# Inverse square roots in the attention and scan part of a decoder layer: starting value on ScalarE, one Newton step on VectorE

## The chip, the cores and the metric

The kernel runs on one core of a Trainium2 chip. The metric is the time of the device for one execution in microseconds (us), the median of several runs. The core has five engines that take their instructions in order, each from a queue of its own, and wait for each other by semaphores: TensorE (PE, with its weight loads as PEld), VectorE (DVE), ScalarE (ACT), GpSimd (POOL) and SyncE (SP, which here only issues DMAs).

## The reference

One layer of a decoder is computed for two groups of requests that share the weights: a prompt of 1024 tokens, and 8 sequences with 4 new tokens each and 4096 cached positions. The parts that the change touches:

```python
def rms_norm(x, g):
    xf = x.astype(jnp.float32)
    y = xf * lax.rsqrt(jnp.mean(xf * xf, axis=-1, keepdims=True) + NORM_EPS)
    return (y * g.astype(jnp.float32)).astype(x.dtype)

def mla_keys(c, w_uk, kn_g):
    return rms_norm(jnp.einsum('...tr,rhd->...thd', c, w_uk), kn_g)

# decoder_layer, in the middle of it
    gdn_out, new_conv, new_s = gdn_mixer(...)      # ends in rms_norm(o, norm_g) * silu(z)
    qn, qr, c, kr = mla_project(...)
    ctx = mla_attend(qn, qr, c, kr, lp['mla_w_uk'], lp['mla_kn_norm'])
    mix = jnp.concatenate([gdn_out, mla_out.astype(gdn_out.dtype)], axis=-1) @ lp['w_out']
```

For the sample group, `mla_attend` makes keys from all 8 x 4096 cached latents (128 numbers each, 8 heads of 64), and each key of each head is divided by the root of its mean square. These roots, and those of the scan's output, are the ones that the change treats.

## The kernel before

The program is one straight run of instructions, made by a tile scheduler that orders each engine's queue by a simulated time line and by the order in the source; GpSimd's order is fixed by hand in the middle of the layer. Products of large size are made of three fp32r matmuls (high and low halves of the operands, `mm3`, lines 125 to 129), which is why nearly all of TensorE's time stands on lines 127 to 129. The stages follow each other: adaLN and first norm, first SwiGLU up and down (to about 900 us), the mixer's input projections with convolution, norms and the triangular inverses (`mixer_in`, to about 1285 us), the heads (`mixer_heads`, about 1285 to 2010 us), output projection, second SwiGLU.

`mixer_heads` (line 2030) is where the change acts. Three pieces of work are woven together there by `together` (line 2017), in a fixed ratio of their steps:

- `mla_prompt_gen`, the prompt's softmax attention, to about 1694 us: tiles `pS`, `pT`, `pa` on TensorE, `pf` and `phi` on ScalarE (lines 1696, 1699), `plo` on GpSimd.
- `scan_gen` with `gdn_sample`, from about 1680 us on: the gated delta scan of the prompt in 17 dependent steps (tiles `sv`, `S`, `so`), and the same recurrence for the sample tokens as a long run of elementwise operations on GpSimd (tiles `gS`, `gt`, all recorded on line 101). `gdn_out` (line 1356) normalises each of the scan's 8 output tiles and the sample's: 9 calls.
- `sample_gen`, attention of the 8 sample sequences over the cache, through the whole of both stages. For each sequence four pieces of cache come by indirect DMA from GpSimd's queue (`fetch`, tile `ck`, line 635; six buffers for the pieces). Each piece is transposed (`kpt`), split (`khi`, `klo`), multiplied to keys (`kraw`), squared on ScalarE (`ksq`, line 2000) and summed per head on VectorE (`kss`, line 2001). After every half of a sequence the function `half` (line 1823) takes the inverse root of 128 x 128 sums, spreads it (`rx`, line 1836, on ScalarE), transposes it (`psr`) and scales the scores with it (`sc`, line 1849). After the second half `soft` makes the softmax and multiplies it with the pieces (`psc`, line 1883), and only then are four buffers free for the next `fetch`. There are 16 halves.

The inverse root itself is `pow_rs` (line 713): one operation for mean and epsilon (line 717), then `rsqrt` (line 704): a starting value by integer arithmetic on the bits (line 707), then three Newton steps of three operations each (lines 709, 710, 711), all on VectorE: 11 operations in a row that depend on each other. In the listings the tile `pv` holds the argument and the temporary, `rsk` the result in `half` (128 x 128), `ors` the result in `gdn_out` (128 x 8). `norm_sums`, `tok_l2`, `head_norm`, `mla_c_post` and `mla_q_finish` use the same functions in other stages.

Of the kernel before, what the change touches and what calls it, by code (L numbers as in the profile page):

```python
# [11 lines left out]
AF = mybir.ActivationFunctionType  # L12
ALU = mybir.AluOpType
# [7 lines left out]
NP = 1024  # L21
NSEQ = 8
NQ = 4
NS = NSEQ * NQ
NT = NP + NS
NB = 4
BW = NT // NB
# [47 lines left out]
class Banks:  # L75


    def __init__(self, **pools):
        self.pools = pools
# [5 lines left out]
class Kernel:  # L85
    def __init__(self, tc, ins, outs, dbg=None):
        self.tc, self.nc, self.i, self.o = tc, tc.nc, ins, outs
        self.dbg = dbg or (lambda name, ap: None)
        self.ctx = ExitStack()
        self.wcount = 0  # L90
        self.hhi, self.hlo, self.nacc, self.nr = ([None] * NB for _ in range(4))

    def pool(self, name, **kw):
# [610 lines left out]
    def rsqrt(self, y, v, t):  # L704

        nc = self.nc
        nc.vector.tensor_scalar(y.bitcast(I32), v.bitcast(I32), -0.5, float(0x5f3759df), ALU.mult, ALU.add)
        for _ in range(3):
            nc.vector.tensor_tensor(out=t, in0=y, in1=y, op=ALU.mult)
            nc.vector.scalar_tensor_tensor(out=t, in0=t, scalar=-0.5, in1=v, op0=ALU.mult, op1=ALU.mult)  # L710
            nc.vector.scalar_tensor_tensor(out=y, in0=t, scalar=1.5, in1=y, op0=ALU.add, op1=ALU.mult)

    def pow_rs(self, out, ss, n, scale, tp, post=None, bufs=2):

        nc = self.nc
        v = tp.tile([P, 2, n], F32, tag=f"pv{n}", name="pv", bufs=bufs)
        nc.vector.tensor_scalar(v[:, 0], ss, scale, EPS, ALU.mult, ALU.add)
        self.rsqrt(out, v[:, 0], v[:, 1])
        if post is not None:
            nc.vector.tensor_scalar(out, out, post, None, ALU.mult)  # L720

# [159 lines left out]
    def taps(self, m, raw, tp):  # L881

        nc = self.nc
        W = NP + 3 + 7 * NSEQ
        sraw = raw[:, NP + 3:].rearrange("p (s r) -> p s r", r=7)
        nc.scalar.copy(raw[:, 0:3], self.zero3)
        nc.scalar.copy(sraw[:, :, 0:3], self.stT[:, m, :].rearrange("p (s j) -> p s j", j=3))
        nc.gpsimd.tensor_copy(self.ncv[:, m, 0:3], raw[:, NP:NP + 3])
        nc.gpsimd.tensor_copy(self.ncv[:, m, 3:27].rearrange("p (s j) -> p s j", j=3), sraw[:, :, 4:7])
        self.done["n"] += 1  # L890
        y = self.r(tp, [P, NTL * P], "cy")
        n = W - 3
        nc.scalar.activation(y[:, :n], raw[:, 0:n], AF.Copy, scale=self.convw[:, 0, m:m + 1])
        for j in range(1, 4):
            nc.vector.scalar_tensor_tensor(out=y[:, :n], in0=raw[:, j:j + n], scalar=self.convw[:, j, m:m + 1], in1=y[:, :n],
                                           op0=ALU.mult, op1=ALU.add)
        nc.scalar.activation(raw[:, :NP], y[:, :NP], AF.Silu)
        nc.scalar.activation(raw[:, NP:NT].rearrange("p (s q) -> p s q", q=NQ), y[:, NP + 3:W].rearrange("p (s r) -> p s r", r=7)[:, :, 0:4], AF.Silu)
        return raw, y

    def tok_l2(self, yt, post, tp, ps):
# [323 lines left out]
    def proj_z(self, m, tp, ps):  # L1225
        nc = self.nc
        zt = self.r(tp, [P, NT], "zt")
        self.proj(lambda b, pp, mm: nc.scalar.activation(zt[:, b * BW:(b + 1) * BW], pp[:, :BW], AF.Silu), ps)
        nc.scalar.dma_start(out=self.z_d[m], in_=zt)

    def mixer_start(self):
# [798 lines left out]
    def mixer_heads(self):  # L2030
        nc, tc, i = self.nc, self.tc, self.i
        self.mix_tiles()
        self.spare = None
        with tc.tile_pool(reuse_waits="tile", name="mc", bufs=1) as mc:
            raw = mc.tile([P, 3, P], F32, name="mraw")
            for n, src in enumerate(("k_causal", "k_causalT", "k_nident")):
                nc.scalar.dma_start(out=raw[:, n, :], in_=i[src])
            self.k_nident = raw[:, 2, :]
            rnd = mc.tile([P, 3, P], F32R, name="mrnd")
            nc.vector.tensor_copy(rnd[:, 0:2], raw[:, 0:2])  # L2040
            nc.vector.tensor_copy(rnd[:, 2], self.ident)
            self.causal, self.causalT, self.identr = (rnd[:, n, :] for n in range(3))
            self.k_eye8 = mc.tile([104, 8], F32, name="k_eye8")
            nc.scalar.dma_start(out=self.k_eye8[96:104], in_=i["k_eye8"])
            self.g_gdn = self.keep.tile([P, 1], F32, name="g_gdn")
            for r in range(2):
                with nc.allow_non_contiguous_dma(reason="a gain per partition"):
                    nc.scalar.dma_start(out=self.g_gdn[64 * r:64 * r + 64, :], in_=i["gdn_norm"][0].rearrange("(d o) -> d o", o=1))
            with tc.tile_pool(reuse_waits="tile", name="sq", bufs=1, side="right") as sq, tc.tile_pool(reuse_waits="tile", name="psq", bufs=PSQ, space=PSUM) as pq:
                smp = self.sample_gen(sq, pq)  # L2050
                with tc.tile_pool(reuse_waits="tile", name="mpp", bufs=1) as mp, tc.tile_pool(reuse_waits="tile", name="psm", bufs=1, space=PSUM) as ps:
                    with tc.manual_schedule(engines={getattr(mybir.EngineType, e) for e in MX}):
                        self.together([(self.mla_prompt_gen(mp, ps), 1)], (smp, RATIO[0]))
                with tc.tile_pool(reuse_waits="tile", name="se", bufs=1) as se, tc.tile_pool(reuse_waits="tile", name="sc", bufs=1) as sp, tc.tile_pool(reuse_waits="tile", name="pss", bufs=SCB, space=PSUM) as ps:
                    with tc.manual_schedule(engines={getattr(mybir.EngineType, e) for e in MY}):
                        self.together([(self.scan_gen(se, sp, ps, "S"), 1), (self.gdn_sample(sp, ps, "S"), RATIO[2])], (smp, RATIO[1]))
                    for _ in smp:
                        pass
# [199 lines left out]
```

## Time and profile before

| | us |
|---|---|
| median of 3 runs | 2859.01 (2853.66 to 2862.34) |
| the profiled execution | 2863.72 |
| its span, first to last instruction | 2861.9 |
| TensorE busy in the span | 2673.6 |
| VectorE busy | 1766.6 |
| ScalarE busy | 1074.2 |
| GpSimd busy | 1083.2 |

The profile shows one execution. A busy time is the sum of what an engine's instructions took; times of instructions that only wait are not in it. Where a group of instructions is listed, the columns are line, engine, operation, written tile and read tiles, shapes, count, busy time in us and mean of one in ns, and behind the bar the idle time of the engine just before, with what ended it. Stretches are given in us from the start of the span. PEclk is the share of TensorE's full clock that was granted.

### The profile page before, as it was taken

The page shows a single profiled execution, that of the slowest core. Times are in us where ns is not written, and L with a number is a line of the kernel's source. Part 1 is how long each engine was busy: PE and PEld are TensorE (multiplying, and loading weights), DVE is VectorE, ACT ScalarE, POOL GpSimd, SP SyncE. Part 2 cuts the span into 40 slices and gives each one's busy share as a digit, 9 for nine tenths or more (in the row PEclk, how much of TensorE's full clock was granted, in tenths as well). Part 3 has the DMA queues.
Part 4 walks back from the last instruction along what each step waited for, and adds up shares of the span by engine and source line. Part 5 has one row for each costly group of instructions (what it writes and reads, how often), then busy time and mean ns, then how long its engine had stood idle before and what let it go on. Part 6 is the DMA issues. An engine that isn't in the chain of part 4 may idle for free.

```text
span 2861.9 us, 53475 instructions
## 1 busy us (share of the span) xinstructions
PE 2673.6 (93%) x21536; PEld 2462.5 (86%) x21536; DVE 1766.6 (62%) x3490; ACT 1074.2 (38%) x2005; POOL 1083.2 (38%) x1032
## 2 busy tenths in 40 slices
PE   4999999989999897799999988998979999999999
PEld 3888989989999787787877866776979999999999
DVE  7644445465574688847767677777585555546555
ACT  5322223211144443324656664543443333322111
POOL 0222222233352555544434466452433333323331
PEclk7999999999999998898999998987979999999999
DMA  7554353243232473432212144222522222224322
GB/s 272 154 163 134 120 162 105 81 161 106 76 109 77 149 206 117 141 110 78 63 42 58 49 96 114 83 64 53 188 82 82 76 87 71 90 82 167 98 76 69
DMA packets 339490, 308.35 MB, mean 108 GB/s; under 512 B 93865, under 2 KB 282017, under 8 KB 336171
## 3 DMA queue, kind: packets, MB, share of 16 engines
q1 hardware_dynamic: 304837, 246.32, 28.4%
q10 hardware_dynamic: 28262, 37.64, 4.1%
q0 software_dynamic: 6144, 20.98, 2.3%
q8 instruction: 169, 2.77, 0.4%
q14 instruction: 78, 0.64, 0.1%
HBM read 229.29 MB, written 75.59 MB: 107 GB/s over the span
## 4 chain that ended last, share of the span: by engine, by line
PE 42%; DVE 8%; issue 5%; POOL 4%; DMA 2%; ACT 1%; SPq 0%; ACTq 0%; POOLq 0%; DVEq 0%
PE po L128 4%; PE po L129 4%; PE po L127 4%; PE pY L127 2%; PE pY L128 2%; PE pY L129 2%; PE kraw L127 2%; PE pX L127 2%; PE pX L128 2%; PE pX L129 1%; PE pZ L127 1%; PE pZ L129 1%; PE pZ L128 1%; PE kraw L129 1%; PE kraw L128 1%
## 5 line engine op out<-in xcount | busy, mean ns | idle before, releaser
L127 PE MATMUL po<-act,whi 128*128 128x264 f32 x1408 | 402.4, 286 | 6.4 <-DVE x L435 4.7
L129 PE MATMUL po<-act,wlo 128*128 128x264 f32 x1408 | 403.2, 286 | 0.0
L128 PE MATMUL po<-act,whi 128*128 128x264 f32 x1408 | 402.0, 286 | 0.0
L435 DVE SCALAR_TENSOR_TENSOR x<-po,modT,x 128x264 f32<-128x264 f32 (+1 forms) x416 | 195.2, 480 | 238.8 <-PE po L129 238.3
L127 PEld LDWEIGHTS po<-act,whi 128*128 128x128 f32 x1408 | 266.8, 189 | 7.1 <-DVE x L435 4.9
L129 PEld LDWEIGHTS po<-act,wlo 128*128 128x128 f32 x1408 | 266.1, 189 | 0.0
L128 PEld LDWEIGHTS po<-act,whi 128*128 128x128 f32 x1408 | 265.9, 189 | 0.0
L370 POOL TENSOR_TENSOR A<-wg,A 128x512 fp32r<-128x512 f32 x84 | 111.0, 1321 | 372.1 <-ACT A L369 372.1
L127 PE MATMUL pp<-hhi,whi 128*128 128x264 f32 (+1 forms) x768 | 223.9, 292 | 4.5 <-DVE nt L354 3.6
L128 PE MATMUL pp<-hlo,whi 128*128 128x264 f32 (+1 forms) x768 | 223.7, 291 | 0.0
L129 PE MATMUL pp<-hhi,wlo 128*128 128x264 f32 (+1 forms) x768 | 221.8, 289 | 0.0
L2001 DVE TENSOR_REDUCE kss<-ksq 128x8 f32<-128x512 f32 x256 | 173.1, 681 | 69.7 <-ACT ksq L2000 67.7
L127 PE MATMUL pX<-B,A 128*128 128x264 f32 x704 | 203.9, 290 | 10.6 <-ACT B L369 9.7
L111 POOL TENSOR_TENSOR wlo<-wraw,whi 128x1024 fp32r<-128x1024 f32 x39 | 97.7, 2510 | 305.2 <-ACT whi L108 305.2
L2000 ACT ACTIVATE ksq<-kraw 128x512 f32<-128x512 f32 x256 | 152.1, 598 | 162.1 <-PE kraw L129 122.2
L128 PE MATMUL pX<-B,A 128*128 128x264 f32 x704 | 202.9, 288 | 8.9 <-DVE B L370 8.9
L128 PE MATMUL pY<-T,S 128*128 128x264 f32 x704 | 200.7, 285 | 1.6 <-DVE T L370 1.5
L129 PE MATMUL pX<-B,A 128*128 128x264 f32 x704 | 201.6, 286 | 0.0
L127 PE MATMUL pY<-T,S 128*128 128x264 f32 x704 | 200.3, 285 | 0.0
L129 PE MATMUL pY<-T,S 128*128 128x264 f32 x704 | 200.2, 284 | 0.0
L1700 POOL TENSOR_TENSOR plo<-pf,phi 128x512 fp32r<-128x512 f32 (+1 forms) x96 | 97.1, 1017 | 187.4 <-ACT phi L1699 169.7
L108 ACT CAST whi<-wraw 128x1024 fp32r<-128x1024 f32 x60 | 61.8, 1048 | 253.6 <-PE po L128 234.1
(538 smaller groups left out, 8305.1 us busy)
## 6 DMA issues: line engine op xcount, KB each, us to landing
adaw<-ada_w SPq DMA_DIRECT2D x72, 512.0 KB
wraw<-ffn_wi SPq DMA_DIRECT2D x46, 512.0 KB
act_d<-cc SPq DMA_DIRECT2D x88, 264.0 KB
wraw<-ffn_wo SPq DMA_DIRECT2D x44, 512.0 KB
wg<-ffn_wi SPq DMA_DIRECT2D x42, 512.0 KB
araw<-act_d ACTq DMA_DIRECT2D x160, 132.0 KB
x_d<-x SPq DMA_DIRECT2D x12, 1056.0 KB
wraw<-w_in SPq DMA_DIRECT2D x23, 512.0 KB
```

Of the source, the lines that this page charges most:

```text
L108: nc.scalar.copy(hi, raw)
L111: eng.tensor_tensor(out=lo, in0=raw, in1=f(hi), op=ALU.subtract)
L127: nc.tensor.matmul(out, whi, ahi, start=first, stop=False, **kw)
L128: nc.tensor.matmul(out, whi, alo, start=False, stop=False, **kw)
L129: nc.tensor.matmul(out, wlo, ahi, start=False, stop=last, **kw)
L370: eng.tensor_tensor(out=lo, in0=src, in1=f(hi), op=ALU.subtract)
L435: nc.vector.scalar_tensor_tensor(out=x[:, d, :n], in0=ps[:, :n], scalar=self.modT[:, m, d, 0:1], in1=x[:, d, :n], op0=ALU.mult, op1=ALU.add)
L1700: nc.gpsimd.tensor_tensor(out=lo[:, off:], in0=pf[:, off:], in1=f(hi[:, off:]), op=ALU.subtract)
L2000: nc.scalar.activation(sq, kr, AF.Square)
L2001: nc.vector.tensor_reduce(out=ss[:, (j * 4 + m) * H:(j * 4 + m + 1) * H], in_=sq.rearrange("p (h d) -> p h d", h=H), axis=AX.X, op=ALU.add)
```

## The change

The functions of `mixer_heads` get another inverse root. `pow_rs` still makes mean plus epsilon on VectorE; then ScalarE takes the logarithm (`AF.Ln`) and the exponential of minus half of it (`AF.Exp`, scale -0.5), and VectorE makes one Newton step instead of a starting value and three steps. This holds for calls after `log_tables`, which `mixer_heads` calls first: the 16 of `half` and the 9 of `gdn_out`. All other calls keep the old way, since `self.logs` is not set yet, or since they call `rsqrt` itself. `log_tables` puts one load of the function table that holds both logarithm and exponential behind all SiLU activations of the stage ahead (they are collected in `self.silus`), and every logarithm is ordered behind this load.

```diff
@@ rsqrt
         for _ in range(3):
-            nc.vector.tensor_tensor(out=t, in0=y, in1=y, op=ALU.mult)
-            nc.vector.scalar_tensor_tensor(out=t, in0=t, scalar=-0.5, in1=v, op0=ALU.mult, op1=ALU.mult)
-            nc.vector.scalar_tensor_tensor(out=y, in0=t, scalar=1.5, in1=y, op0=ALU.add, op1=ALU.mult)
+            self.newton(y, v, t)
+
+    def newton(self, y, v, t):
+        nc = self.nc
+        nc.vector.tensor_tensor(out=t, in0=y, in1=y, op=ALU.mult)
+        nc.vector.scalar_tensor_tensor(out=t, in0=t, scalar=-0.5, in1=v, op0=ALU.mult, op1=ALU.mult)
+        nc.vector.scalar_tensor_tensor(out=y, in0=t, scalar=1.5, in1=y, op0=ALU.add, op1=ALU.mult)
+
+    def log_tables(self):
+
+        with ExitStack() as e:
+            for inst in self.silus:
+                e.enter_context(self.tc.issue_after(inst))
+            self.logs = self.nc.scalar.preload_act_table_set("natural_log_exp_and_others").ins
@@ pow_rs
         nc.vector.tensor_scalar(v[:, 0], ss, scale, EPS, ALU.mult, ALU.add)
-        self.rsqrt(out, v[:, 0], v[:, 1])
+        if self.logs:
+
+            with self.tc.issue_after(self.logs):
+                nc.scalar.activation(v[:, 1], v[:, 0], AF.Ln)
+            nc.scalar.activation(out, v[:, 1], AF.Exp, scale=-0.5)
+            self.newton(out, v[:, 0], v[:, 1])
+        else:
+            self.rsqrt(out, v[:, 0], v[:, 1])
@@ mixer_heads
         self.spare = None
+        self.log_tables()
```

(The two places that make a SiLU, in `taps` and `proj_z`, append their instruction to `self.silus`.) The lines of the new program are shifted by 4 in `newton` (713 to 715) and by 18 behind `pow_rs`: 717 becomes 728, 1836 becomes 1854, 2001 becomes 2019. The new logarithm stands on line 732, the exponential on 733, the table load on 722.

Since the scheduler orders the queues anew, the queues of `mixer_heads` change in many places, though the work of each engine apart from the roots is the same. Three places are shown.

First, ScalarE's queue at the start of `mixer_heads`. `zt` is the last SiLU of the stage ahead, `z_d` its store, `qk` and `vhi` belong to the prompt's attention, `sn` to the new tokens' scores. Before:

```order
L1228 ACTIVATE zt<-pp 128x264 x4
L1229 DMA z_d<-zt 128x1056
L1607 CAST qk_14488<-pqk 96x512 x2
L1627 CAST vhi_14477<-vld 128x8x64
L1607 CAST qk_14491<-pqk 96x512 x2
L1979 CAST khi<-kpt 128x512
L1816 ACT_TABLE_LOAD
L1816 ACTIVATE sn<-sn 32x32
```

and of the change:

```order
L1246 ACTIVATE zt<-pp 128x264 x4
L722 ACT_TABLE_LOAD
L1247 DMA z_d<-zt 128x1056
L1625 CAST qk_14489<-pqk 96x512 x2
L1645 CAST vhi_14478<-vld 128x8x64
L1625 CAST qk_14492<-pqk 96x512 x2
L1997 CAST khi<-kpt 128x512
L1834 ACTIVATE sn<-sn 32x32
```

The table load has moved from its place ahead of `sn` to a place ahead of the last store of `z_d`; there is one load in this stretch in either program, and 12 in each of the two as a whole.

Second, VectorE's queue at the root of the fourth half, in the attention stage. `mx`, `mxt` and `qk` belong to the prompt's attention. Before, the first 12 of 20 rows (behind them the second Newton step ends and the third follows in the same manner):

```order
L717 TENSOR_SCALAR pv<-kss 128x128
L2001 TENSOR_REDUCE kss<-ksq 128x8
L1630 TENSOR_TENSOR mx<-mx 128x4
L707 TENSOR_SCALAR rsk<-pv 128x128
L709 TENSOR_TENSOR pv<-rsk 128x128
L710 SCALAR_TENSOR_TENSOR pv<-pv 128x128
L711 SCALAR_TENSOR_TENSOR rsk<-pv,rsk 128x128
L2001 TENSOR_REDUCE kss<-ksq 128x8
L709 TENSOR_TENSOR pv<-rsk 128x128
L2001 TENSOR_REDUCE kss<-ksq 128x8
L710 SCALAR_TENSOR_TENSOR pv<-pv 128x128
L1635 TENSOR_TENSOR mxt<-pmx,k_eye_14429 8x512 x2
```

and of the change, the whole root and the row behind it:

```order
L728 TENSOR_SCALAR pv<-kss 128x128
L1639 TENSOR_REDUCE mx<-pS 128x1
L1648 TENSOR_TENSOR mx<-mx 128x4
L1998 TENSOR_TENSOR klo<-kpt,khi 128x512
L713 TENSOR_TENSOR pv<-rsk 128x128
L714 SCALAR_TENSOR_TENSOR pv<-pv 128x128
L715 SCALAR_TENSOR_TENSOR rsk<-pv,rsk 128x128
L2019 TENSOR_REDUCE kss<-ksq 128x8
```

Seven of the eleven operations of the root are gone, and the row of the first Newton operation (`pv<-rsk`) now waits for ScalarE. Over the 16 halves, 138 other rows of VectorE stood between the first and the last operation of a root; now 45 stand between the first operation and the Newton step, and 24 within the step.

Third, ScalarE's queue at the same half. Before, up to the row `rx` that takes the result:

```order
L2000 ACTIVATE ksq<-kraw 128x512 x3
L1638 CAST qk_14490<-mxt 8x512 x2
L1842 COPY krT<-pkt 128x512
L1979 CAST khi<-kpt 128x512
L1696 ACTIVATE pf<-pT 128x512
L1699 CAST phi<-pf 128x512
L1696 ACTIVATE pf<-pT 128x512
L1836 COPY rx<-rsk 128x512
```

and of the change:

```order
L732 ACTIVATE pv<-pv 128x128
L1997 CAST khi<-kpt 128x512
L733 ACTIVATE rsk<-pv 128x128
L1714 ACTIVATE pf<-pT 128x512
L2018 ACTIVATE ksq<-kraw 128x512
L1717 CAST phi<-pf 128x512
L1854 COPY rx<-rsk 128x512
```

The logarithm (`pv<-pv`) waits for VectorE's row of line 728, and whatever stands behind it on ScalarE waits with it. Over the 16 halves 18 rows of other work stand between logarithm and exponential; over the 9 calls of `gdn_out` it is 3.

More of the change, by code (lines that the diff above doesn't have):

```diff
@@ L89, in __init__ @@
         self.ctx = ExitStack()
-        self.wcount = 0
+        self.wcount, self.logs, self.silus = 0, None, []
         self.hhi, self.hlo, self.nacc, self.nr = ([None] * NB for _ in range(4))
@@ L897, in taps @@
         nc.scalar.activation(raw[:, :NP], y[:, :NP], AF.Silu)
-        nc.scalar.activation(raw[:, NP:NT].rearrange("p (s q) -> p s q", q=NQ), y[:, NP + 3:W].rearrange("p (s r) -> p s r", r=7)[:, :, 0:4], AF.Silu)
+        self.silus.append(nc.scalar.activation(raw[:, NP:NT].rearrange("p (s q) -> p s q", q=NQ), y[:, NP + 3:W].rearrange("p (s r) -> p s r", r=7)[:, :, 0:4], AF.Silu).ins)
         return raw, y
@@ L1227, in proj_z @@
         zt = self.r(tp, [P, NT], "zt")
-        self.proj(lambda b, pp, mm: nc.scalar.activation(zt[:, b * BW:(b + 1) * BW], pp[:, :BW], AF.Silu), ps)
+        self.proj(lambda b, pp, mm: self.silus.append(nc.scalar.activation(zt[:, b * BW:(b + 1) * BW], pp[:, :BW], AF.Silu).ins), ps)
         nc.scalar.dma_start(out=self.z_d[m], in_=zt)
```

## The prediction

> **What bounds the kernel now.** I read the busy times first, then the two stages in which the change acts.
>
> ```profile
> span 2861.9 us, 53475 instructions
> PE 2673.6 (93%) x21536; PEld 2462.5 (86%) x21536; DVE 1766.6 (62%) x3490; ACT 1074.2 (38%) x2005; POOL 1083.2 (38%) x1032
> core 0: us, PE busy (x) PEld busy (x) DVE busy (x) ACT busy (x) POOL busy (x), PEclk, DMA share, GB/s
> 1285.00:1694.00 409.00, 392.64 (x2292) 320.81 (x2290) 287.46 (x531) 251.63 (x495) 187.40 (x211) 0.97 0.24 60
> 1694.00:2010.00 316.00, 283.53 (x3032) 217.15 (x3032) 237.94 (x521) 143.06 (x288) 159.63 (x183) 0.87 0.32 87
> ```
>
> TensorE bounds the whole, but not evenly. In the attention stage (first stretch) it is idle for 409.00 - 392.64 = 16.4 us only. In the scan stage (second) it is idle for 32.5 us, VectorE is busy for 75%, and the granted clock is 0.87: an engine that waits in short turns. Ahead of 1285 us and behind 2010 us the change moves no computation, so the forecast is a matter of these 725 us.
>
> Next, who ends the waits there.
>
> ```profile
> POOL ck L635 <- PE psc L1883: 95.0, 5, 33.0
>   DVE rsk L711: 14.6, 13
> PE pS L1472 <- DVE sv L1459: 7.1, 5, 2.2
> ```
>
> The first row is from the waits of GpSimd: it stood 95.0 us before gathers of cache pieces, until `psc` had used up the old ones. So `sample_gen` is a closed loop: gather, transposes, keys, sums, root, scores, softmax, `psc`, next gather. The second is from the listing of `rx` (line 1836): ScalarE stood idle 13 times, 14.6 us, for the last Newton operation. The third is the longest wait of TensorE in the scan stage: VectorE was late with `sv` of the recurrence.
>
> How long one root takes in the loop is seen in order of time, its first and its last operation in the fourth half:
>
> ```profile
> 1458.16 0.21 DVE L717 TENSOR_SCALAR pv<-kss 128x128 f32<-128x128 f32 x1
> 1467.82 0.84 DVE L711 SCALAR_TENSOR_TENSOR rsk<-pv,rsk 128x128 f32<-128x128 f32 x1
> ```
>
> From 1458.16 to 1468.66, 10.5 us for 11 operations, since other work of VectorE stands between them.
>
> **What is removed.** 25 calls change; two sorts of 128x128 and 128x8:
>
> ```profile
> L711 DVE SCALAR_TENSOR_TENSOR rsk<-pv,rsk 128x128 f32<-128x128 f32 x48 | 24.9, 518 | 0.7
> L709 DVE TENSOR_TENSOR pv<-rsk 128x128 f32<-128x128 f32 x48 | 23.9, 499 | 0.6
> L710 DVE SCALAR_TENSOR_TENSOR pv<-pv 128x128 f32<-128x128 f32 x48 | 22.5, 469 | 0.9
> L707 DVE TENSOR_SCALAR rsk<-pv 128x128 int32<-128x128 int32 x16 | 6.3, 396 | 0.2
> L710 DVE SCALAR_TENSOR_TENSOR pv<-pv 128x8 f32<-128x8 f32 x27 | 9.2, 351 | 0.3
> L709 DVE TENSOR_TENSOR pv<-ors 128x8 f32<-128x8 f32 x27 | 7.0, 270 | 0.3
> L711 DVE SCALAR_TENSOR_TENSOR ors<-pv,ors 128x8 f32<-128x8 f32 x27 | 6.1, 236 | 0.1
> L707 DVE TENSOR_SCALAR ors<-pv 128x8 int32<-128x8 int32 x9 | 3.0, 342 | 0.1
> ```
>
> Line 707 goes, and two of three rounds of 709 to 711. In `half`: 6.3 + 2/3 x (24.9 + 23.9 + 22.5) = 53.8 us, 3.36 us a call. In `gdn_out`: 3.0 + 2/3 x (9.2 + 7.0 + 6.1) = 17.9 us. Together 71.7 us of VectorE. Which stage they leave is told by the calls of line 707 in each:
>
> ```profile
> 1285.00:1694.00 409.00, 4.26 (x9) 0.97 0.24 60
> 1694.00:2010.00 316.00, 5.06 (x16) 0.87 0.32 87
> ```
>
> Nine halves in the first: 9 x 3.36 = 30.3 us of its 287.46. Seven halves and the nine of `gdn_out` in the second: 7 x 3.36 + 17.9 = 41.4 us of 237.94.
>
> These durations hold something that is not arithmetic.
>
> ```profile
> L709 DVE TENSOR_TENSOR pv<-rsk x48: 270/292/3932, 1340.4 to 1988.0; 128x128 f32<-128x128 f32 x48
> L709 DVE TENSOR_TENSOR pv<-ors x27: 145/166/1005, 1760.5 to 1998.9; 128x8 f32<-128x8 f32 x27
> 1766.14 1.00 DVE L709 TENSOR_TENSOR pv<-ors 128x8 f32<-128x8 f32 x1
> 1765.04 4.13 POOL L101 TENSOR_TENSOR gS<-gS,gqk 128x512 f32<-128x512 f32 x4
> ```
>
> The median is 292 ns where the mean is 499, and an operation on 8 columns that can take 145 ns took 1.00 us at 1766.14, while GpSimd ran `gS`. Line 2001, which reads one input, took 681 ns on average and hardly varies. So some 40% of the 71.7 us (1 - 292/499) is waiting beside GpSimd; without it 42 us would be removed. I take 71.7: the operation that follows is mostly one that the trace does not show slowed.
>
> The Trainium skill has a rule for this: "SBUF — State Buffer", section "Who interferes with whom", says that VectorE with two inputs in SBUF and a GpSimd operation that reads SBUF exclude each other for the whole operation, that a reduction never does, and that ScalarE waits for nobody. The trace agrees by the 1.00 us above. By this rule the 71.7 us go whole, since ScalarE's two operations cannot be held up; if the wait were handed on to the next operation, 42 us would go, and the gain below would shrink to about 42/71.7 of it, 16 us.
>
> **What is added.** On ScalarE 32 operations of 128x128 and 18 of 128x8. Neither is in the trace; the nearest rows are
>
> ```profile
> L1696 ACT ACTIVATE pf<-pT 128x128 f32<-128x128 f32 x16 | 4.5, 278 | 3.9 <-PE pT L1694 2.9 <-POOL plo L1700 0.6 <-PE pqk L1605 0.2
> L1816 ACT ACTIVATE sn<-sn 32x32 f32<-32x32 f32 x1 | 0.2, 228 | 0.0
> L2000 ACT ACTIVATE ksq<-kraw 128x512 f32<-128x512 f32 x256 | 152.1, 598 | 162.1 <-PE kraw L129 122.2 <-DVE kss L2001 10.2 <-PE po L1486 6.2
> L2001 DVE TENSOR_REDUCE kss<-ksq 128x8 f32<-128x512 f32 x256 | 173.1, 681 | 69.7 <-ACT ksq L2000 67.7
> ```
>
> 32 x 0.278 + 18 x 0.228 = 13.0 us. ScalarE is idle for 157 us in the first stage and 173 us in the second, so I count this at nothing but for its place in the root's own path; uncovered it would be 13 us. Bounds: 0 and 13.
>
> The table load moves. It stands ahead of the store of `z_d`, and that store is on the chain that ended last:
>
> ```profile
> 1285.71 2.64 DMA z_d<-zt
> 1309.84 1.28 ACT L1816 ACT_TABLE_LOAD   x1
> ```
>
> The load took 1.28 us; VectorE and TensorE begin the stage behind the store, so 1.3 us are added. At its old place ScalarE had been idle before, so nothing is certain to come back there. The Trainium skill, "ScalarE: Activation LUTs", section "What ACT_TABLE_LOAD costs", puts a switch at 2.66 us with a drain; the load's 1.28 us agrees, the drain has no row here, and by the page the sum would lose another 1.4 us.
>
> **The sum.** Attention stage: bounds are 0 (TensorE is in order and full) and its idle 16.4 us. VectorE's load falls from 70% to 63%, which shortens many short waits and not all; I take half, 8 us.
>
> Scan stage: bounds are 0 and the 41.4 us that leave VectorE. The loop gives a value between. One root now holds its 11 operations, 0.355 (line 717, its mean) + 0.396 + 3 x 1.486 = 5.2 us, and 138/16 = 8.6 other rows of about 0.68 us, 5.9 us; 11.1 us, near the 10.5 us seen. After, 0.355 + 1.486 of its own and 69/16 = 4.3 others, 2.9 us: 4.8 us, if ScalarE's part fits under the rows between. So 6 us less for each turn of the loop, and three turns end in the stage (`psc` of the last three sequences): 18 us. The scan's own chain gains beside it, as VectorE is in both; a stretch of the chain of waits shows how much of it can be roots:
>
> ```profile
> by line: DVE pv L710 23.9%; DVE kss L2001 19.1%; DVE pv L709 18.3%; DVE rsk L711 10.6%; DVE ors L711 7.1%; PE pss L128 6.1%; DVE klo L1980 5.4%; ACT ksq L2000 4.7%; PE kraw L129 3.4%; DVE sU L1411 3.4%; issue 1.3%
> ```
>
> (1764 to 1777 us: 60% of 13 us, 7.8 us, though this is the worst place.) I take 20 us, near the loop's value.
>
> 8 + 20 - 1.3 = 26.7 us. The profiled execution took 2863.7 us, its span 2861.9 with 1.8 around it; 2863.7 - 26.7 = 2837.0. It lay 4.7 us above the median of the runs, 2859.0, so the forecast is 2837.0 - 4.7 = **2832 us**.
>
> Nothing else moves work: `norm_sums` and the roots of the stage ahead keep their operations, the collected SiLUs cost nothing, GpSimd's order is by hand, and SP's queue moves two loads of the output weights ahead of the loads of `x`, which costs less than those two loads take (0.5 MB each).
>
> **Rivals.**
>
> *Slower, by ScalarE's place in the root.* Each call now waits twice across engines: the logarithm holds ScalarE's queue until line 728 is done, and the Newton step holds VectorE's queue, with the `kss` rows and the recurrence's `sv` behind it, until the exponential. The path is 0.278 + 0.278 us and 18/16 = 1.1 rows of other work between, each worth 598 ns and a wait of 122.2/256 = 0.48 us for `kraw`: 0.56 + 1.1 x 1.08 = 1.75 us. The cover is 45/16 = 2.8 rows of VectorE, 1.9 us. On average it fits; but these rows are mostly `kss`, which itself waits for ScalarE (67.7 us). If none of it covers, 16 x 1.75 + 9 x (0.46 + 0.36) = 35 us are lost against 27 won: 2859 + 8 = **2867 us**. It decides from 26.7/25 = 1.07 us exposed per call. Against it: `rx` already waited in this manner, for 14.6 us in all.
>
> *Hidden.* TensorE's queue is fixed, and its waits in the scan are for many producers; its longest, 7.1 us, is for `sv`, not a root. Then the loop's slack is taken up by `kraw` and the recurrence, and at most 12 us remain: 2847 to 2860 us, middle **2855 us**. For it: 96% busy in the first stage. Against: the 95.0 us of the gathers.
>
> *Larger.* The whole of 41.4 us in the scan and 12 us in attention, because shorter waits also bring the clock back from 0.87: 41.4 + 12 - 1.3 = 52 us, **2807 us**. Against: it asks every removed operation to have been on the path.
>
> **How the numbers follow.** Forecast (12 to 40 us won) 0.58, larger 0.12, hidden 0.18, slower 0.12. About 0.3%, 8.6 us, is what a measurement of this kernel can tell from no change. Faster: 0.58 + 0.12 + 0.05 of the hidden case = 0.75. Same: 0.13 of it and 0.02 of the slower = 0.15. Slower: 0.10. The range takes in the bounds of both stages, 16.4 + 41.4 - 1.3 = 56.5 us below 2859, that is 2803, and the whole hidden case with a loss of the load on top, 2862; the rest of the slower case, 0.10, and less of the larger one, lie outside.
>
> **What would show it.** Of the changed kernel: VectorE's busy time in the two stages lower by about 70 us; from line 728 to the last row of line 715 about 5 us; the gathers' waits for `psc` shorter, and `mixer_heads` ending near 1985 us on the span's clock; PEclk in the scan above 0.87. The slower rival would show as idle time of VectorE before line 713, ended by line 733, above 25 us. I would be wrong on the mechanism if VectorE's time fell as said and the stage did not shorten.

## The result, and the profile after

The changed kernel took 2835.57 us (median of 4 runs, 2833.71 to 2838.29) against 2859.49 us before: a ratio of 0.992, 95% interval [0.9902, 0.9938]. By the ratio that is 23 us less (17.7 to 28.0 by its interval); the medians lie 23.9 us apart. Measured again in a later batch of six runs, the ratio was 0.9927 [0.9909, 0.9944]. The forecast was 2832 us, 27 us less.

The page of the profiled execution, span and busy times:

```profile
span 2830.8 us, 53341 instructions
PE 2659.3 (94%) x21536; PEld 2459.8 (87%) x21536; DVE 1716.5 (61%) x3315; ACT 1082.2 (38%) x2055; POOL 1082.9 (38%) x1032
```

VectorE fell by 50.1 us of busy time and the span by 31.1 us; this execution (2833.71 us) is the fastest of its four, and that of before (2863.7 us) was slower than its runs (2853.66 to 2862.34), so the pair shows more than the medians do. For the place, both traces are cut at events of the program: the last store of `z_d` is issued, the last `psc` of the fourth sequence ends (the attention stage), the last `psc` of all ends (the scan stage). Columns as in the prediction's windows (us, busy times, PEclk, DMA). Before:

```profile
0.00:1285.70 1285.70, 1173.69 (x9509) 1103.23 (x9509) 761.21 (x1589) 428.84 (x801) 460.74 (x462) 0.96 0.43 135
1285.70:1674.70 389.00, 378.35 (x2220) 310.35 (x2219) 274.12 (x507) 241.79 (x476) 171.31 (x195) 0.97 0.23 59
1674.70:2005.60 330.90, 294.54 (x3070) 225.00 (x3070) 247.87 (x537) 150.28 (x300) 174.49 (x198) 0.88 0.32 84
2005.60:2861.90 856.30, 827.00 (x6741) 823.88 (x6740) 483.38 (x857) 253.28 (x428) 276.64 (x178) 0.97 0.31 98
```

and after:

```profile
0.00:1283.10 1283.10, 1176.20 (x9508) 1106.71 (x9508) 762.79 (x1589) 428.88 (x801) 460.82 (x462) 0.95 0.43 136
1283.10:1663.70 380.60, 372.84 (x2214) 309.13 (x2213) 251.13 (x450) 243.25 (x493) 170.18 (x195) 0.97 0.24 59
1663.70:1972.00 308.30, 283.29 (x3077) 220.50 (x3077) 221.54 (x420) 156.61 (x335) 176.24 (x198) 0.90 0.35 93
1972.00:2830.80 858.80, 826.96 (x6744) 823.51 (x6740) 481.03 (x856) 253.44 (x428) 275.64 (x177) 0.97 0.30 97
```

Attention 389.00 to 380.60, 8.4 us less; scan 330.90 to 308.30, 22.6 less; what lies ahead and behind differs by 2.6 and 2.5 us in opposite directions. In the scan half of the gain is TensorE's own busy time (294.54 to 283.29 for as many matmuls), at a granted clock of 0.90 against 0.88. Why the clock was higher is not shown: in the table below it does not simply follow the time for which TensorE stands still.

The root's rows in the two stages, grouped by line and shape (count | busy us, mean ns | idle before them):

```profile
L728 DVE TENSOR_SCALAR pv<-kss 128x128 f32<-128x128 f32 x16 | 13.6, 851 | 0.3
L713 DVE TENSOR_TENSOR pv<-rsk 128x128 f32<-128x128 f32 x16 | 8.6, 539 | 1.6 <-ACT rsk L733 1.6
L732 ACT ACTIVATE pv<-pv 128x128 f32<-128x128 f32 x16 | 5.0, 311 | 14.7 <-DVE pv L728 14.6
L733 ACT ACTIVATE rsk<-pv 128x128 f32<-128x128 f32 x16 | 4.9, 308 | 0.2
L732 ACT ACTIVATE pv<-pv 128x8 f32<-128x8 f32 x9 | 1.8, 207 | 3.3 <-DVE pv L728 3.3
L733 ACT ACTIVATE ors<-pv 128x8 f32<-128x8 f32 x9 | 1.8, 205 | 0.2
```

The crossing is cheap: VectorE sat idle for 1.6 us before line 713, and what ScalarE waits in front of line 732 it had waited in front of `rx` before. But line 728 takes 13.6 us in this execution, where the same operation took 5.7 before:

```profile
L717 DVE TENSOR_SCALAR pv<-kss 128x128 f32<-128x128 f32 x16 | 5.7, 355 | 0.3
```

The longest of these 16 operations stood beside a chain of four operations of GpSimd and ended 0.09 us behind the last of them:

```profile
1822.57 3.36 DVE L728 TENSOR_SCALAR pv<-kss 128x128 f32<-128x128 f32 x1
1821.81 4.03 POOL L101 TENSOR_TENSOR gS<-gS,gqk 128x512 f32<-128x512 f32 x4
```

All seven that took over 0.3 us ended 0.08 or 0.09 us behind an operation of GpSimd.

The waits of GpSimd for the loop, in the changed kernel:

```profile
POOL ck L635 <- PE psc L1901: 70.7, 4, 31.9
```

95.0 us before. The time from line 728 to the last Newton operation is 5.3 us on average over the 16 halves, from 10.2.

### The profile page after: what moved, and what is told of

It is laid out like the page before. It is cut to its first block, busy times and chain, and to the rows that moved or that the text cites. A ratio compares the mean times of both kernels' runs of the same rounds, so it can differ in the third digit from the quotient of the medians.

```text
span 2830.8 us, 53341 instructions
## 1 busy us (share of the span) xinstructions
PE 2659.3 (94%) x21536; PEld 2459.8 (87%) x21536; DVE 1716.5 (61%) x3315; ACT 1082.2 (38%) x2055; POOL 1082.9 (38%) x1032
## 4 chain that ended last, share of the span: by engine, by line
PE 43%; DVE 5%; issue 3%; POOL 3%; DMA 2%; ACT 1%; POOLq 0%; DVEq 0%; ACTq 0%; SPq 0%
PE po L127 4%; PE po L128 4%; PE po L129 4%; PE pY L127 2%; PE pY L128 2%; PE pY L129 2%; PE kraw L127 2%; PE pX L127 2%; PE pX L128 2%; PE pX L129 2%; PE pZ L127 1%; PE pZ L129 1%; PE kraw L128 1%; PE pZ L128 1%; PE kraw L129 1%
## 5 line engine op out<-in xcount | busy, mean ns | idle before, releaser
L128 PE MATMUL pY<-T,S 128*128 128x264 f32 x704 | 200.7, 285 | 2.1 <-DVE T L370 2.1
```

Source lines behind the costliest of these rows:

```text
L128: nc.tensor.matmul(out, whi, alo, start=False, stop=False, **kw)
```

## The experiments

The prediction added up the shorter way of a root through the sampling loop (called A below). The rivals tested are that VectorE's busy time counts wherever it stands (B), that the changed order of TensorE's queue brings the gain (C; when the program is built the queues are laid out again, and every kernel here has an order of its own), and, in the third batch, that what counts is how long VectorE's operations are held up beside GpSimd's (D).

Most verdicts need the same stretch of the trace, the three turns of the loop in the scan stage from the end of the fourth sequence's `psc` to the end of the seventh's. All in one table, from the windows between those two events in each kernel's profile; the column "held" is worked out from the trace: over the operations of VectorE, what each took above the fastest tenth of its group (same tile, operation and shape, over all these traces), where that is over 0.1 us. Before and with the change, each operation that counts in it ran beside one of GpSimd.

| kernel | ratio to before, 95% | three turns, us | VectorE busy, us | held, us | TensorE busy, us | PEclk |
|---|---|---|---|---|---|---|
| before | 1 | 238.4 | 185.6 | 30.2 | 216.6 | 0.91 |
| change | 0.992 [0.9902, 0.9938] | 216.4 | 163.7 | 21.4 | 205.2 | 0.95 |
| change, again | 0.9927 [0.9909, 0.9944] | 221.7 | 162.0 | 19.7 | 209.2 | 0.94 |
| only `half` | 0.997 [0.9955, 0.9986] | 227.2 | 176.9 | 30.4 | 209.1 | 0.93 |
| only `gdn_out` | 1.0001 [0.9988, 1.0015] | 226.7 | 179.9 | 29.0 | 209.5 | 0.95 |
| load behind the root | 0.9992 [0.9979, 1.0005] | 230.8 | 186.5 | 32.0 | 211.6 | 0.93 |
| three Newton rounds | 0.9996 [0.9984, 1.0007] | 233.0 | 183.5 | 30.3 | 210.9 | 0.96 |
| guess, one round | 0.9949 [0.9931, 0.9967] | 216.9 | 164.3 | 20.8 | 205.7 | 0.95 |
| no Newton round | 0.9928 [0.991, 0.9946] | 216.5 | 154.9 | 18.4 | 207.2 | 0.95 |
| all in ScalarE | 0.9917 [0.9896, 0.9938] | 205.0 | 142.7 | 5.9 | 200.7 | 0.98 |
| all in ScalarE, again | 0.9928 [0.9912, 0.9945] | 216.2 | 144.7 | 8.1 | 206.7 | 0.95 |
| reductions behind the root | 0.9947 [0.993, 0.9964] | 225.8 | 173.0 | 16.3 | 214.0 | 0.92 |
| late root | 0.9917 [0.9902, 0.9932] | 220.8 | 162.2 | 19.6 | 206.0 | 0.96 |

The length is that of one profiled execution; the same program gave 216.4 and 221.7, and 205.0 and 216.2, so differences of 5 to 10 us in that column alone decide nothing. Ratios are of 6 to 12 runs of the kernel, but for the first measurement of the change; the runs of before in one batch differ among themselves (2845.57 to 2868.66 us in that of "all in ScalarE"), so a ratio need not be the quotient of two medians. The two rows for the kernel before and after, of which the table gives a part:

```profile
1674.70:1913.10 238.40, 216.55 (x2297) 166.22 (x2297) 185.60 (x378) 115.97 (x231) 138.14 (x157) 0.91 0.34 94
1663.70:1880.10 216.40, 205.19 (x2303) 160.92 (x2303) 163.66 (x302) 119.78 (x254) 138.23 (x157) 0.95 0.38 105
```

**Only one of the two sorts of roots.** Edit, for the halves; `n == H` instead of `n == P` for `gdn_out`:

```diff
-        if self.logs:
+        if self.logs and n == P:
```

> Only the 16 roots of `half` (128x128) are made the new way; the 9 of `gdn_out` keep the guess and three Newton rounds. Theory A (the shorter way of the root through the sampling loop is what gains): nearly all of the gain stays, 20 to 24 us, ratio 0.992 to 0.993, and the scan stage (from the last psc of the attention stage to the last psc of all) is about 312 us long, against 331 before and 308 with the whole change. Theory B (what counts is VectorE's busy time, wherever it leaves): 53.8 of the 71.7 us that were to go, so 0.75 of 24 us, 18 us, ratio 0.9937. Theory C (the gain is that of a changed order of TensorE's queue): TensorE's order here is nearly that of the whole change, so the whole 24 us, ratio 0.992.

> Only the 9 roots of `gdn_out` (128x8) are made the new way. Theory A: these roots are not in the sampling loop, so 0 to 4 us, ratio 0.9985 to 1.000. Theory B: 17.9 of 71.7 us, 6 us, ratio 0.998. Theory C: TensorE's order is nearly that of the kernel before, ratio 1.000.

Measured: 2849.51 against 2858.38 us, ratio 0.997, and 2858.07, ratio 1.0001. For the halves all three theories miss: they bring 9 us instead of 18 to 24. `gdn_out` alone brings nothing, as C and A allowed; B's 0.998 lies just below the interval [0.9988, 1.0015]. So B misses twice, and no theory says why both together bring 23. C falls with the halves: the trace shows TensorE's matmuls in the order of the change up to 1760 us, and behind it in another order in about a dozen short places only, but most of the gain is missing. In the three turns of these single executions the parts add up, 11.2 and 11.7 us, together 22.0 with the change (16.7 in its second execution). What `gdn_out` alone had won there it gave back in the last turn of the loop; before and with `gdn_out` alone:

```profile
1913.10:2005.60 92.50, 77.99 (x775) 58.79 (x774) 62.27 (x159) 34.30 (x69) 36.34 (x42) 0.80 0.25 59
```

```profile
1894.60:1998.60 104.00, 84.26 (x758) 64.21 (x758) 63.61 (x132) 36.55 (x77) 40.40 (x42) 0.70 0.29 71
```

It took 11.5 us more; 6.3 us of that is TensorE's own busy time, at a granted clock of 0.70 against 0.80. Why this turn became longer was not settled.

The kernel with the halves alone shows what such a root costs in a bad place. Its timeline, VectorE, GpSimd and the TensorE row that came late (start, duration, ... [idle before it <- releaser]):

```profile
1851.38 4.06 POOL L101 TENSOR_TENSOR gt<-gS,gqk 128x512 f32<-128x512 f32 x4
...
1852.49 0.97 DVE L713 TENSOR_TENSOR pv<-ors 128x8 f32<-128x8 f32 x1
1853.49 0.97 DVE L714 SCALAR_TENSOR_TENSOR pv<-pv 128x8 f32<-128x8 f32 x1
1854.38 0.67 DVE L2019 TENSOR_REDUCE kss<-ksq 128x8 f32<-128x512 f32 x1
...
1855.15 0.60 ACT L2018 ACTIVATE ksq<-kraw 128x512 f32<-128x512 f32 x1 [4.71 <-DVE kss L2019]
...
1856.85 0.76 PE L127 MATMUL pss<-khi,qpad 128*128 128x512 f32 x1 [4.83 <-ACT ksq L2018]
```

Two operations on 8 columns take 0.97 us each, one per operation of GpSimd's chain; `kss` behind them is late, so `ksq` on ScalarE, which needs its buffer back, waits 4.71 us, and TensorE 4.83. (This is one of the few places where TensorE's order is not that of the change, so not all of it need be the root's.)

**The load of before, put behind the root.** Into `pow_rs`, behind the Newton step (`a`, `b` are the two halves of `v`):

```diff
+            nc.vector.tensor_scalar(b.bitcast(I32), a.bitcast(I32), -0.5, float(0x5f3759df), ALU.mult, ALU.add)
+            for _ in range(2):
+                nc.vector.tensor_tensor(out=b, in0=a, in1=a, op=ALU.mult)
+                nc.vector.scalar_tensor_tensor(out=b, in0=b, scalar=-0.5, in1=a, op0=ALU.mult, op1=ALU.mult)
+                nc.vector.scalar_tensor_tensor(out=b, in0=b, scalar=1.5, in1=a, op0=ALU.add, op1=ALU.mult)
```

> The whole change, and behind each root's last Newton operation seven operations of VectorE of the same sizes as those that were removed, on a scratch half of the root's own tile that nobody reads. VectorE's load is that of before, the root's result is ready as early as with the change. Theory A: the gain stays, but for what the seven operations delay behind them: 2836 to 2845 us, ratio 0.992 to 0.995. Theory B: the gain is gone, ratio 0.999 to 1.001, and VectorE is busy for about 1767 us again. Theory C: TensorE's order is close to that of the change, so the gain stays, ratio 0.992.

Measured: 2856.66 us, ratio 0.9992. The three turns:

```profile
1666.40:1897.20 230.80, 211.58 (x2311) 164.18 (x2307) 186.48 (x378) 119.48 (x253) 139.07 (x158) 0.93 0.36 98
```

The roots were as early as with the change (5.1 us on average from line 728 to the last row of the root), and the gain is gone. That is as B has it, and A, which expected 0.992 to 0.995, falls.

**A late root without load on VectorE.**

```diff
+            for _ in range(5 if n == P else 0):
+                nc.scalar.copy(v[:, 1], v[:, 1])
             nc.scalar.activation(out, v[:, 1], AF.Exp, scale=-0.5)
```

> The whole change, and in the 16 roots of `half` five copies on ScalarE between logarithm and exponential, so that the root is about as late as before the change (some 10 us from line 728 to the last Newton operation) while VectorE has no more to do. Theory A (the root's way through the sampling loop gains): 5 us lost for each turn, three turns and more in the scan stage, 15 us or more: ratio 0.997 or above. Theory B: the gain stays but for 25 us more of ScalarE, ratio 0.992 to 0.995.

Measured: 2839.56 against 2862.33 us, ratio 0.9917, beside the change's own 0.9927 on the same chip. The roots took 8.6 us on average over the 16 halves, two thirds of the way back to 10.2; over the six halves of the three turns it was 7.2 us, where it was 5.1 with the change and 10.7 before. ScalarE had 24.1 us more:

```profile
L734 ACT COPY pv<-pv 128x128 f32<-128x128 f32 x80 | 24.1, 301 | 0.8
```

No loss was measured. The delay in the three turns is smaller than was planned: 2.1 us a root, which at one root for each turn, as the prediction counts, would cost about 6 us by A. The two intervals leave room for a loss of about 4 us (an estimate from their widths). So this speaks against A, less sharply than the kernel with the load behind the root does: the time from `kss` to `rsk` is at most a small part of what gains.

**Three Newton rounds behind the exponential, and one round behind the guess.** The first keeps the crossing and nearly all of VectorE's work; the second drops the crossing and keeps VectorE's guess:

```diff
-            self.newton(out, v[:, 0], v[:, 1])
+            for _ in range(3):
+                self.newton(out, v[:, 0], v[:, 1])
```

```diff
-            with self.tc.issue_after(self.logs):
-                nc.scalar.activation(v[:, 1], v[:, 0], AF.Ln)
-            nc.scalar.activation(out, v[:, 1], AF.Exp, scale=-0.5)
+            nc.vector.tensor_scalar(out.bitcast(I32), v[:, 0].bitcast(I32), -0.5, float(0x5f3759df), ALU.mult, ALU.add)
             self.newton(out, v[:, 0], v[:, 1])
```

> The change with three Newton rounds behind logarithm and exponential instead of one: VectorE is spared only the guess (9.4 us), and the root goes across to ScalarE and back. Theory A: the root's way is longer than before by the two activations and their waits, less the guess, about 0.6 to 1.5 us for each of 16 halves: 0 to 12 us slower than before, ratio 1.000 to 1.004. Theory B: 9.4 of 71.7 us less load, 3 us faster, ratio 0.999. Theory C: TensorE's order is unlike both, so nothing is foretold. The rival of the prediction (ScalarE's place in the root costs more than 1.07 us a call) would show as over 10 us lost here.

> VectorE's guess and one Newton round, without logarithm and exponential (two of three Newton rounds are left out of the computation). VectorE has 9.4 us more than with the change, ScalarE 13.5 us less, and the root stays on one engine. If ScalarE's place in the root costs nothing (the forecast's step: its two operations fit under the rows between), the time is that of the change or up to 3 us above it: ratio 0.992 to 0.993. If the crossing costs time (the slower rival in a mild form, 0.3 us or more for each of 25 calls), this one is faster than the change by 5 to 10 us: ratio 0.989 to 0.990.

Measured: 0.9996 (2857.91 us) and 0.9949 (2840.57 against 2855.69 us). With the crossing and the old load the time is that of before, as B has it, and the rival's loss of over 10 us is not there. Without the crossing the kernel is not faster than the change, as it would be if the crossing cost time; its ratio is a little above the 0.992 to 0.993 that was expected, and its interval [0.9931, 0.9967] overlaps that of the change.

**Less than one Newton round.** First the Newton step is taken away; then the scaling as well (it stays for the calls that keep the old way, and a new constant tile `eps` holds the epsilon; both left out here):

```diff
-        nc.vector.tensor_scalar(v[:, 0], ss, scale, EPS, ALU.mult, ALU.add)
         if self.logs:
...
-                nc.scalar.activation(v[:, 1], v[:, 0], AF.Ln)
+                nc.scalar.activation(v[:, 1], ss, AF.Ln, bias=self.eps, scale=scale)
             nc.scalar.activation(out, v[:, 1], AF.Exp, scale=-0.5)
-            self.newton(out, v[:, 0], v[:, 1])
```

> The change without its Newton step (left out of the computation; the exponential's result is taken as it is). VectorE loses another 75 operations, 33 us of busy time in the two stages. Theory A and B both: a further gain of about the same share as the change had of its own (24 us for 62 us of VectorE, so 13 us): 2823 us, ratio 0.987 to 0.989. If the chain's next limit (gathers, kraw, the recurrence) is reached already: 0 to 4 us more, ratio 0.991 to 0.992.

> As without the Newton step, and the scaling and the added epsilon are done inside the logarithm's activation (scale and bias), so VectorE does nothing for these 25 roots: 42 us less than with the change, and one crossing between engines less. Further gain over the kernel without Newton step: 17 us of VectorE at the same rate, 7 us, plus 25 shorter waits: ratio 0.984 to 0.987. If the next limit is reached already: the same as without the Newton step within 2 us.

> The kernel with scale and epsilon inside the logarithm's activation and no Newton step, once more, beside the change on one chip. The first time its ratio was 0.9917 [0.9896, 0.9938] with a median of 2824.9 us against 2855.7. If it beats the change: ratio below 0.990, and 5 to 12 us under the change's median here. If not: within 3 us of it.

Measured: 0.9928 without the Newton step; 0.9917 and, again, 0.9928 without any work of VectorE in these roots. The further gains that B forecast (0.987 to 0.989, and 0.984 to 0.987) did not come. In the second batch, beside the change (0.9927) on the same chip, the medians are 2840.13 and 2841.58 us: no difference that can be told. The three turns of the first of the two executions without VectorE:

```profile
1661.60:1866.60 205.00, 200.69 (x2323) 158.86 (x2324) 142.72 (x259) 121.15 (x255) 137.87 (x157) 0.98 0.41 111
```

TensorE is busy for 200.69 of 205.00 us, at a clock of 0.98; before it was 216.55 of 238.40 at 0.91. So none of these kernels beats the change by a measurable amount. For the kernel without VectorE that does not prove that its roots gain nothing. Its scan stage was shorter than that of the change, 304.0 against 312.4 us in the second batch (293.3 against 308.3 in the first executions of the two), but it lost time where the roots have no part. In the second batch, from 128 us behind the last `psc` to the end, the change and then the kernel without VectorE:

```profile
2104.00:2834.20 730.20, 715.73 (x5856) 713.93 (x5856) 394.19 (x707) 194.47 (x340) 221.99 (x139) 0.99 0.29 89
2098.00:2834.10 736.10, 720.45 (x5856) 718.43 (x5856) 394.57 (x707) 194.38 (x340) 221.89 (x139) 0.98 0.28 89
```

The same 5856 matmuls took 5.9 us more, and the first execution of this kernel shows it too (736.3 us). The one part of the edit that lies outside the roots is the tile `eps`; whether it is the cause was not tried. The kernel without the Newton step has no such tile and no such loss (859.8 us behind the last `psc`, 858.8 with the change), and it too gained nothing from 9 us less of VectorE in the three turns.

**Work that cannot be held beside GpSimd.**

```diff
             self.newton(out, v[:, 0], v[:, 1])
+            for _ in range(9 if n == P else 7):
+                nc.vector.tensor_reduce(out=v[:, 1, 0:1], in_=v[:, 0], axis=AX.X, op=ALU.add)
```

> The changed kernel itself, beside the three others of this batch on one chip: ratio 0.990 to 0.994, as before.

> The whole change, and behind each root nine reductions of 128x128 (seven of 128x8) on VectorE into a scratch column that nobody reads: about as much undisturbed work as the seven operations of the run with the load behind the root, but of a sort that the traces show hardly lengthened beside GpSimd (kss lies between 0.67 and 0.69 us). Theory B (VectorE's busy time counts): the gain is mostly gone, ratio 0.997 to 1.000. Theory D (what counts is the time for which VectorE's operations are held beside GpSimd's chains gS and gt): the gain stays, ratio 0.992 to 0.995.

Measured: 2848.34 us, ratio 0.9947 [0.993, 0.9964], between the change beside it (2841.58, 0.9927 [0.9909, 0.9944]) and the kernel with the old operations behind the root (0.9992 [0.9979, 1.0005]). The three turns:

```profile
1672.50:1898.30 225.80, 214.02 (x2307) 165.72 (x2308) 172.98 (x390) 119.57 (x253) 137.52 (x157) 0.92 0.37 101
```

The ratio lies in the range that D gave (0.992 to 0.995), at its upper end, and outside B's (0.997 to 1.000). But B's range took VectorE to be as busy as with the old operations, and it was not: 173.0 us in the three turns, between 163.7 and 186.5. VectorE's work without the holding is as much as with the old operations (busy less held 157 and 155 us), its holding half as much (16.3 and 32.0 us), and less of the gain is lost; the two intervals lie apart, though they come from different batches. By D alone nothing should be lost, since no more is held than with the change; the medians of the two lie 6.8 us apart, but their intervals overlap, so what the undisturbed work costs is open. What orders most rows, from before down to the change, is VectorE's busy time with the holding in it; that is a reading of the table, and the parts above (the halves, `gdn_out`) do not follow it in the ratio.

**The table load ahead of the store.**

```diff
-            self.logs = self.nc.scalar.preload_act_table_set("natural_log_exp_and_others").ins
+            for _ in range(4):
+                for name in ("silu_and_others", "natural_log_exp_and_others"):
+                    self.logs = self.nc.scalar.preload_act_table_set(name).ins
```

> The change with eight alternating table loads instead of one at the place ahead of the last store of z_d on ScalarE's queue, 8 x 1.28 = 10.3 us. If the store waits for the loads, as the prediction took it, the store of z_d is issued 10 us behind the last SiLU and the attention stage starts 9 us later. If a store is issued past a load in work, as one load in the trace of the change suggests (load at 1283.13, store at 1283.14), the store starts less than 1.3 us behind the last SiLU, or behind the last but one load, and only the first activation of the next stage (qk, 1.5 us behind the store) is late.

ScalarE and its DMA queue in the changed kernel, and then with eight loads:

```profile
1282.72 0.39 ACT L1246 ACTIVATE zt<-pp 128x264 f32<-128x264 f32 x1 [2.51 <-PE pp L129]
1283.13 1.28 ACT L722 ACT_TABLE_LOAD   x1
1283.14 0.33 ACTq L1247 DMA_DIRECT2D z_d<-zt  x1
1284.65 1.06 ACT L1625 CAST qk<-pqk 96x512 fp32r<-96x512 f32 x2 [0.23 <-PE pqk L1623]
```

```profile
1283.23 0.39 ACT L1248 ACTIVATE zt<-pp 128x264 f32<-128x264 f32 x1 [2.51 <-PE pp L129]
1283.64 5.15 ACT L724 ACT_TABLE_LOAD   x4
1287.57 0.33 ACTq L1249 DMA_DIRECT2D z_d<-zt  x1
1288.79 5.15 ACT L724 ACT_TABLE_LOAD   x4
```

With one load the store is issued 0.01 us behind the load's start and 0.03 us behind the last SiLU (1282.72 + 0.39), as early as before the change, where it was 0.03 us too. With eight it is issued 3.95 us behind the SiLU: behind three loads, with five still to end, and not behind all 10.3 us. Neither of the two expectations had this. The time of this single run was 2833.19 us. So the one load costs nothing at this place: the next activation (`qk`) begins behind its end, and 0.23 us later still, when TensorE has its product.

## Why the prediction came out

**The number was right, its longest sum was not.** 23 us measured, 27 forecast, with the stages near theirs: attention 8.4 for 8 us, scan 22.6 for 20 in the profiled pair (18.5 in the second profile of the change, 330.9 to 312.4 us).

**What was removed** came out smaller. "I take 71.7", said the prediction, since the operation that follows is mostly one not slowed. VectorE's busy time fell by 23.0 and 26.3 us in the two stages, 49.3 (52.1 in the second profile of the change). The removed rows themselves were sized well: guess and Newton steps sum to 103.8 us before and 33.7 after, 70.1 less. The rest was lost in three ways. First, sums of rows overstate: the records of VectorE's operations overlap by some hundredths of a microsecond, and in the two stages the sum of all rows fell by 59 us where the busy time fell by 49. Second, the operation that could take over the wait stands in the changed code itself: the 16 calls of line 728, with one input, went from 5.7 to 13.6 us, 7.9 us. The Trainium skill has a reason, "SBUF — State Buffer", section "Who interferes with whom": beside the rule that the prediction weighed it names `tensor_scalar` among the operations that can take both ports and then exclude GpSimd. The 3.36 us that the longest of these operations took agree; the prediction used only the half of the page on two inputs. But the 7.9 us are not steady: in the second profile of the changed kernel these calls took 7.6 us, and with `gdn_out` alone, where `half` keeps the old root, 14.6. So how much of the wait is handed on is not shown. Third, the rows of other work took 3.9 us more. The bound of 42 us was nearer than 71.7, but the wait handed on, for which it stood, explains about half of the difference at most.

**The table load, +1.3 us**, was nothing: the store does not wait for one load. The further 1.4 us for a drain that the Trainium skill adds ("ScalarE: Activation LUTs", section "What ACT_TABLE_LOAD costs") do not appear either; eight switches in a row took 10.3 us, 1.29 each.

**The scan's 20 us rest on a step that failed**: "6 us less for each turn of the loop, and three turns end in the stage". The root's way did shrink as worked out (10.2 to 5.3 us, said 4.8), and the gathers waited 24 us less. But with it short and the load restored nothing was won, and with that way lengthened again to 8.6 us (7.2 in the three turns) no loss was measured. The gain went with VectorE's load: `kss` and `klo` are its operations, `ksq` and the recurrence wait for it, and in the three turns it was busy for 163.7 us instead of 185.6. By which of these waits the load lengthens the loop was not separated, and why the two sorts of roots gain less singly than together stays open. That two different sums gave nearly the same figure is chance.

**Attention, "half of 16.4"**, was a choice between bounds and came out (8.4). The kernels with the old load behind the root, with three Newton rounds and with the reductions took 383.9, 384.4 and 388.6 us there, so at least part of it goes with the load; how much of the stage's gain is load was not separated further.

**Slower rival**: VectorE idle before line 713 was 1.6 us, not above 25; three Newton rounds behind the crossing gave 0.9996. It fell. **Hidden**: at most 12 us were to remain; the halves alone came out so (9 us), the whole did not. **Larger** (52 us) asked every removed operation to be on the path; with another 21 us gone from the three turns (all in ScalarE) the time did not fall further, though that kernel lost 5.9 us where the roots have no part.

## What to carry to other kernels

Where an engine is at 75% beside a full TensorE, test whether its load or the length of the way counts before adding up either: put the removed work behind the result, and put a delay into the result without the work. Measure in the trace that the delay came out as long as it was meant to be. Do not take a sum of rows for busy time (59 and 49 us here), and profile the same program twice before reading a row's change as an effect (13.6 and 7.6 us for line 728). Parts of a change can be worth less singly than together. And when a further step brings nothing, look whether it lost time in stages that it should not touch.

## What the runs showed of the hardware

A store on ScalarE's queue was issued while table loads ahead of it had not ended: one load delayed it by nothing, eight by three loads (3.95 us), with five loads still to end. Eight alternating table loads took 1.29 us each, with no gap. An operation of VectorE with one input (line 728, 128x128, 0.23 us at the median) took up to 3.36 us beside GpSimd's `gS` and ended 0.09 us behind it, while reductions of 128x512 kept to 0.65 to 0.69 us. The same program differed by 5 to 11 us over the same three turns from one profiled execution to the next; with all roots in ScalarE the granted clock of the two was 0.98 and 0.95.
